# Gates one tick sooner, one product less in six pauses, and a last output block finished transposed

## The chip, the core and the metric

The kernel runs on one core of one Trainium2 chip. The metric is the device time of one execution in microseconds, the median of several runs. The engines are TensorE (PE: matrix products; PEld: its weight loads), VectorE (DVE), ScalarE (ACT), GpSimd (POOL) and SyncE (SP); DMA queues are fed by SP, ACT and POOL.

## The reference

A decoder trunk of two layers on 256 tokens of width 2048, all in float32. Layer 0 mixes by gated linear attention, layer 1 by sliding-window attention with sinks, and each mixer is followed by an MLP whose hidden width is 8192:

```python
def sqrelu_mlp(h, w1, w2):
    u = jax.nn.relu(h @ w1)
    return (u * u) @ w2

log_a = jax.nn.log_sigmoid((glr @ w_g2 + b_g).astype(f32)) / GLA_GATE_TAU
bc = jnp.cumsum(to_chunks(log_a, dk), axis=-2)
...
decay = jnp.exp(jnp.where(causal, diff, -jnp.inf))
attn = jnp.einsum('bhid,bhjd,bhijd->bhij', qi, ki, decay)
...
h = h + mixer(rmsnorm(h, norm_mix[layer]))
h = h + sqrelu_mlp(rmsnorm(h, norm_mlp[layer]), mlp_w1[layer], mlp_w2[layer])
```

The last line quotes the two updates of a layer in short; `mixer` stands for either of the two.

## The kernel before

Every weight block of 512 x 512 comes by a DMA into a tile (`ws`, `wx` or `wy`, 128 x 4 x 512) and is split by `halve` into a high half `wh` (a cast on ScalarE, L114) and a low half `wl` (a subtraction on VectorE, L115), each in two pieces of 128 x 1024. A product then takes, for each of four k, three matrix products: high activations by `wh`, high by `wl`, low by `wh`. The activations were split in the same way before. The residual stream lies in four tiles `xs[c]` of 512 columns with the tokens on the partitions, in two halves t of 128 tokens.

Python code emits the instructions, and a tile scheduler with priorities (`tc.high_priority`) orders each engine's instructions. Within the emission there is a calendar: `later(n, fn)` puts a piece of work n ticks ahead, and each chunk of a large product calls `tick()`.

In layer 0 the calendar spreads the gate computation over the large products. `gate` (four calls, a half hh of the columns and a half t of the tokens each) makes log_a; `cumsum` (four calls from tick `CS` on) its running sums by products with a triangular matrix; `levels(hp, n)` starts, for each pair of heads hp, the Gram products of seven levels (64, 32, ... 1) of the decay's blocks. A level computes its factors on VectorE (L582, L590), GpSimd and ScalarE into a tile `mlev`, and two ticks later `level_gram` multiplies them on PE into a bank of the two `ms` banks, from which VectorE's masked copy L604 takes the result. `diag(hp)` does the same for the diagonal products (`ms<-qT,kTt`), with the masked copy L614.

An MLP runs in four quarters g of the hidden width. In each, products with w1 fill the activations, and then `seven` forms the product with w2 for n = 0 and n = 1, in a scheme that replaces eight block products by seven of sums of blocks plus a few plain ones. Its names: `load` issues a weight block's DMA on SP; `more(x, i, j)` adds another block to tile x by an accumulating DMA on GpSimd (L1004); `product(b, o, ws)` splits `ws` and multiplies with operand o into bank b; `plain(i, j, b0, b1)` is a block product without a sum, one bank for each half of the tokens; `add` (L1041) and `sub` (L1042) bring banks into v or `xs`. At the very end (g = 3, n = 1 of the last MLP) `send(c, t, b, k)` transposes columns of `xs[c]` on PE (L1050), copies them on ScalarE (L1052) and issues the DMA to the output (L1053), which is stored with the tokens on the fast axis. `c0` and `c1` are the column blocks 2 and 3 there; `x11, x21` are the two halves of tokens of c0, `x12, x22` those of c1.

`pause` (L950 to L954) is called by the calendar once in each quarter and issues fp32 products of `ident` by a column of `ones` into an `ms` bank; its result is not used.

Of the kernel before, what the change touches and what calls it, by code (L numbers as in the profile page):

```python
# [16 lines left out]
P = 128  # L17
T = 256
NT = T // P
D = 2048  # L20
KT = D // P
C = 512
# [11 lines left out]
WS = 3  # L34
WHL = 4
WPRI = 60
QPRI = 100
LV = 2
WARM = 11
CS = 14  # L40
RS = 4
MX = 2
COMB = (1, 3)
# [6 lines left out]
def yoco_kernel(ctx: ExitStack, tc: tile.TileContext, x, norms, mlp_w1, mlp_w2, a_w_in, w_glr, w_gate, a_g_o, a_w_o,  # L50
                kv_w_k, kv_w_v, kv_g_k, b_w_q, b_g_q, b_sinks, b_w_o, out):
    nc = tc.nc
# [4 lines left out]
    wp = ctx.enter_context(tc.tile_pool(name="wp", bufs=2))  # L57
# [5 lines left out]
    def bank(shape, tag, dtype=F32):  # L63
        return ps[tag].tile(shape, dtype, name=tag, tag=tag)
# [7 lines left out]
    def later(n, fn):  # L72
        due.setdefault(now[0] + n, []).append(fn)

    def tick():
        now[0] += 1
        for fn in due.pop(now[0], ()):
            fn()

    def mm(o, l, r, start=True, stop=True, **kw):  # L80
        nc.tensor.matmul(o, lhsT=l, rhs=r, start=start, stop=stop, **kw)  # L81
# [23 lines left out]
    def halve(ws, o=C, n=2):  # L105

        whs = [wp.tile([P, 2, C], F32R, name="wh", tag="wh", bufs=WHL) for _ in range(2)]
        wl = wp.tile([P, 4, C], F32R, name="wl", tag="wl", bufs=WS)
        with tc.high_priority(offset=WPRI):
            for k in range(0, 4, n):  # L110
                wh = whs[k // 2]
                js, ks = slice(k % 2, k % 2 + n), slice(k, k + n)
                w = ws[k // 2] if isinstance(ws, list) else ws[:, ks, :o]
                nc.scalar.copy(out=wh[:, js, :o], in_=w)  # L114
                nc.vector.tensor_sub(out=wl[:, ks, :o], in0=w, in1=wh.bitcast(F32)[:, js, :o])  # L115
        return [(whs[k // 2][:, k % 2], wl[:, k]) for k in range(4)]
# [98 lines left out]
    class Seven:  # L215
# [16 lines left out]
        def load(self, i, j):  # L232
            ws = wp.tile([P, 4, C], F32, name="ws", tag="ws", bufs=WS)
            with tc.high_priority(offset=WPRI):
                nc.sync.dma_start(out=ws, in_=self.block(i, j))
            return ws
# [28 lines left out]
        def plain(self, i, j, b0, b1):  # L265
            halves = halve(self.load(i, j))
            ps_ = [self.use(b) for b in (b0, b1)]
            for k in range(4):
                wh, wl = halves[k]
                for t in range(NT):  # L270
                    p, st = ps_[t]
                    a, l = self.token(i, t)
                    mm(p, a[:, k], wh, st and k == 0, False, skip_group_check=True)
                    mm(p, a[:, k], wl, False, False, skip_group_check=True)
                    mm(p, l[:, k], wh, False, k == 3, skip_group_check=True)
                if k % 2:
                    tick()
# [90 lines left out]
    tail, last = {}, []  # L368
# [175 lines left out]
    def gate(t, hh):  # L544
        cs = slice(hh * C, (hh + 1) * C)
        zp = bank([P, C], "ms")
        for i, w in enumerate((wgh, wgl)):
            mm(zp, zin[:, t * P:(t + 1) * P], w[:, cs], i == 0, i == 1)
        e = g2.tile([P, C], F32, name="e", tag="og")
        nc.scalar.activation(out=e, in_=zp, func=AF.Abs)  # L550
        nc.scalar.activation(out=e, in_=e, func=AF.Exp, scale=-1.0)
        nc.scalar.activation(out=e, in_=e, func=AF.Ln, bias=1.0)
        nc.vector.scalar_tensor_tensor(out=la[t][:, cs], in0=zp, scalar=0.0, in1=e, op0=ALU.min, op1=ALU.subtract)
# [109 lines left out]
    glr(bank([P, 2, T], "tp"), 5)  # L663
    for hh in range(2):
        for t in range(NT):
            later(7 + 4 * hh + 2 * t, lambda t=t, hh=hh: gate(t, hh))
    for c2 in range(4):
        later(CS + c2, lambda c2=c2: cumsum(c2))
    go_all(gemm_q(0))
# [269 lines left out]
    def mlp(w1, w2, act, r, gains):  # L939
# [7 lines left out]
        wide_tags.sort()  # L947
        vs = [mp.tile([P, C], F32, name=f"v{n}", bufs=1) for n in range(2)]

        def pause():  # L950

            pt = small()
            for i in range(2):
                mm(pt[:, i:i + 1], ident, ones[:, 0:1])  # L954

        def new_ops():
# [29 lines left out]
        def seven(w, n, op, us, g, acts, gains, sq, nr):  # L986
# [21 lines left out]
            def use(b):  # L1008
                if b in banks:
                    return banks[b], False  # L1010
                banks[b] = bank([P, C], "ms" if b in "EF" else "acc")
                return banks[b], True

            def product(b, o, ws):
                p, st = use(b)
                halves = halve(ws)
                for k in range(4):
                    wh, wl = halves[k]
                    mm(p, op[o][:, 0, k], wh, st and k == 0, False, skip_group_check=True)
                    mm(p, op[o][:, 0, k], wl, False, False, skip_group_check=True)  # L1020
                    mm(p, op[o][:, 1, k], wh, False, k == 3, skip_group_check=True)
                tick()
                return p
# [20 lines left out]
            def send(c, t, b=0, k=4, queue=nc.scalar if n == 0 else nc.sync):  # L1044

                if c not in left:
                    left[c] = mp.tile([P, 4, T], F32, name="xt", tag="u")
                tp = bank([P, 4, P], ("tp", "ms")[t * n])
                for j in range(k):
                    nc.tensor.transpose(out=tp[:, j, :], in_=xs[c][:, t, (b + j) * P:(b + j + 1) * P], identity=ident)  # L1050
                o, r, tt = left[c][:, b:b + k, t * P:(t + 1) * P], c * C + b * P, slice(t * P, (t + 1) * P)
                nc.scalar.copy(out=o, in_=tp[:, :k])  # L1052
                queue.dma_start(out=out[r:r + k * P, tt].rearrange("(k p) t -> p k t", p=P), in_=o)  # L1053

            def done(c):
# [10 lines left out]
                if len(turn) == NC4:  # L1066
                    later(1, lambda: rstd_of(nr, sq))


            x = load(mp, "wx", 2, 0, 0)  # L1070
            p = product("A", 0, x)
# [15 lines left out]
            with tc.high_priority(offset=WPRI):  # L1087
                nc.vector.tensor_add(out=y, in0=y, in1=b12)
            sub(x22, product("C", 6, y))
            for i in (2, 3):  # L1090
                plain(i, 0, "A", "C", i == 2)
            add(v, product("D", 5, x))
# [7 lines left out]
                nc.vector.tensor_add(out=x, in0=x, in1=b21)  # L1100
            product("A", 1, b21)
            add(x11, banks["A"])
            if g == n + 2 == 3 and not gains:

                p, _ = use("C")
                halves = halve(x)
                for b in range(2):
                    bs = slice(b * T, (b + 1) * T)
                    for k in range(4):
                        wh, wl = (w[:, bs] for w in halves[k])  # L1110
                        mm(p[:, bs], op[3][:, 0, k], wh, False, False, skip_group_check=True)
                        mm(p[:, bs], op[3][:, 0, k], wl, False, False, skip_group_check=True)
                        mm(p[:, bs], op[3][:, 1, k], wh, False, k == 3, skip_group_check=True)
                    tick()
                    add(x21[:, bs], p[:, bs])
                send(c0, 0)
                for b in range(2):
                    send(c0, 1, 2 * b, 2, nc.scalar)
                return
            add(x21, product("C", 3, x))  # L1120
            if g == 3:
                done(c0)
# [2 lines left out]
        for g in range(4):  # L1125
            w = w2[g * D:(g + 1) * D]
            us, op, uf = {}, None, {}
            later(1 if g else RS + 3, pause)
            for c in range(NC4):
                if c >= 2:  # L1130
                    us[c] = new_act()
                elif c == 0:
                    op = new_ops()
                ms = {}

                def evac_u(f, acc, c=c, ms=ms):
                    if f % 2 == 0:
                        ms[0] = mp.tile([P, 2, T], F32, name="m", tag="m")
                    if f == 0:
                        uf[c] = mp.tile([P, 4, T], F32, name="u", tag="u")  # L1140
                    m, j = ms[0], f % 2
                    nc.scalar.copy(out=m[:, j], in_=acc[:, 1])
                    nc.vector.tensor_add(out=m[:, j], in0=acc[:, 0], in1=m[:, j])
                    if j == 0:
                        return
                    bs = slice(f - 1, f + 1)
                    nc.vector.scalar_tensor_tensor(out=m, in0=m, scalar=0.0, in1=rb2, op0=ALU.max, op1=ALU.mult)
                    nc.scalar.activation(out=uf[c][:, bs], in_=m, func=AF.Square)
                    if c >= 2:
                        ah, al, _ = us[c]  # L1150
                        nc.scalar.copy(out=ah[:, bs], in_=uf[c][:, bs])
                        nc.vector.tensor_sub(out=al[:, bs], in0=uf[c][:, bs], in1=ah.bitcast(F32)[:, bs])
                    elif f == 3:
                        combine(op, c, uf)

                go_all(gemm_wide(piece(w1, g * D + c * C), act, evac_u))
            for n in range(2):
                seven(w, n, op, us, g, acts, gains, sq, nr)
# [241 lines left out]
```

## Time and profile before

| what | value |
|---|---|
| median of 3 runs | 2036.23 us (2035.28 to 2036.71) |
| the profiled execution, its own time | 2036.59 us |
| span in its profile | 2034.9 us |
| busy PE | 2023.3 us, 99% of the span |
| busy DVE | 1546.8 us, 76% |
| busy ACT | 1202.9 us, 59% |
| busy POOL | 161.4 us, 8% |
| granted TensorE clock over the span | 1.0 |

Busy time is the time in which at least one instruction of the engine is under way. The span is the time from the first to the last instruction that the profile shows; what lies around it is in the execution's own time alone. The granted clock is the share of full speed (2.4 GHz) that TensorE was given; 0.5 is its lower level of 1.2 GHz.

### The profile page before, as it was taken

What the parts mean: (1) busy time and instruction counts of PE and PEld (TensorE: products, weight loads), DVE (VectorE), ACT (ScalarE), POOL (GpSimd) and SP (SyncE); (2) the same over time, 40 slices, a digit from 0 to 9 for tenths busy, and PEclk for the clock granted to TensorE, in tenths of its full rate; (3) what the DMA queues carried; (4) which work ended last, traced back from release to release, by engine and by line L of the source; (5) the groups of instructions that cost most, each with busy time, mean ns of one, the idle gap of its engine ahead of it and who ended that gap; (6) DMA issues with size and microseconds to landing.
All of it is one profiled execution on the core that took longest, in us unless ns stands there. A gap on an engine that the chain in (4) does not pass through costs nothing.

```text
span 2034.9 us, 26993 instructions
## 1 busy us (share of the span) xinstructions
PE 2023.3 (99%) x10578; PEld 1716.3 (84%) x10578; DVE 1546.8 (76%) x1796; ACT 1202.9 (59%) x1638; POOL 161.4 (8%) x175
## 2 busy tenths in 40 slices
PE   9999999999999999999999999999999999999999
PEld 9988888888888888888887877788888888888887
DVE  6698787867866876786798676876876786787777
ACT  6746666656555655555566677655655555555555
POOL 2151110000000000000001121000000000000000
PEclk9999999999999999999999999999999999999999
DMA  8445876676965785776666543775785786687575
GB/s 287 160 140 179 224 207 207 188 255 179 267 229 190 225 267 186 213 242 228 186 207 188 166 145 123 200 258 186 227 264 191 200 255 218 188 255 230 186 224 148
DMA packets 219280, 423.15 MB, mean 208 GB/s; under 512 B 7328, under 2 KB 17840, under 8 KB 219152
## 3 DMA queue, kind: packets, MB, share of 16 engines
q1 hardware_dynamic: 194224, 376.59, 54.3%
q0 software_dynamic: 21568, 42.81, 12.2%
q10 hardware_dynamic: 3360, 2.01, 0.3%
q8 instruction: 83, 1.36, 0.3%
q14 instruction: 45, 0.37, 0.1%
HBM read 419.29 MB, written 2.10 MB: 207 GB/s over the span
## 4 chain that ended last, share of the span: by engine, by line
PE 91%; DVE 4%; ACT 2%; DMA 1%; issue 1%; POOL 0%; SPq 0%; ACTq 0%; DVEq 0%; POOLq 0%
PE acc L81 58%; PE ms L81 22%; PE tp L81 10%; DVE wl L115 1%; ACT sc L1283 1%; DMA ws<-in_a_w_in_dram 1%; DMA wx<-in_mlp_w_dram 1%; PE tp L831 0%; ACT wh L114 0%; DVE sc L1293 0%; PE tp L1215 0%; DVE st L1277 0%; DVE act L340 0%; PE tp L701 0%; DVE po L1310 0%
## 5 line engine op out<-in xcount | busy, mean ns | idle before, releaser
L115 DVE TENSOR_TENSOR wl<-ws,wh 128x1024 fp32r<-128x1024 f32 x600 | 737.7, 1238 | 277.9 <-ACT wh L114 274.6
L114 ACT CAST wh<-ws 128x1024 fp32r<-128x1024 f32 x600 | 629.0, 1052 | 448.9 <-PE acc L81 285.9
L81 PE MATMUL acc<-wh,act 128*128 128x512 f32 x1696 | 544.5, 394 | 0.5 <-DVE xs L1042 0.3
L81 PE MATMUL acc<-act,wh 128*128 128x512 f32 (+1 forms) x1536 | 453.7, 359 | 0.0
L81 PEld LDWEIGHTS acc<-wh,act 128*128 128x128 f32 x1696 | 317.5, 188 | 69.0 <-issue 2.0
L81 PE MATMUL acc<-act,wl 128*128 128x256 f32 x1280 | 355.1, 279 | 0.1
L81 PE MATMUL acc<-wl,act 128*128 128x512 f32 x848 | 330.2, 390 | 0.0
L81 PEld LDWEIGHTS acc<-act,wh 128*128 128x128 f32 x1536 | 272.6, 189 | 43.5
L115 DVE TENSOR_TENSOR wl<-wx,wh 128x1024 fp32r<-128x1024 f32 x160 | 193.5, 1222 | 87.6 <-ACT wh L114 85.2
L114 ACT CAST wh<-wx 128x1024 fp32r<-128x1024 f32 x160 | 167.9, 1054 | 143.4 <-PE acc L81 81.1
L81 PEld LDWEIGHTS acc<-act,wl 128*128 128x128 f32 x1280 | 241.3, 189 | 1.6 <-DVE wl L402 0.3
L81 PE MATMUL tp<-act,wh 128*128 128x512 f32 x528 | 204.6, 392 | 0.8 <-DVE wh L518 0.8
L81 PE MATMUL ms<-act,wh 128*128 128x512 f32 x512 | 202.0, 394 | 0.0
L81 PEld LDWEIGHTS acc<-wl,act 128*128 128x128 f32 x848 | 159.4, 188 | 32.8 <-issue 1.4
L81 PE MATMUL ms<-wh,act 128*128 128x512 f32 x512 | 163.4, 390 | 0.0
L81 PE MATMUL ms<-act,wl 128*128 128x256 f32 x512 | 143.4, 280 | 0.0
L1004 POOL DMA_DIRECT2D wx<-in_mlp_w_dram x32 | 41.2, 1288 | 1268.2 <-DVE wl L115 1252.5
L81 PE MATMUL tp<-act,wl 128*128 128x256 f32 x512 | 140.7, 275 | 0.0
L81 PE MATMUL acc<-wh,ops 128*128 128x512 f32 (+1 forms) x392 | 123.6, 386 | 0.3 <-ACT wh L114 0.3
L81 PE MATMUL acc<-wh,op 128*128 128x512 f32 x384 | 123.4, 389 | 0.0
L81 PEld LDWEIGHTS tp<-act,wh 128*128 128x128 f32 x528 | 99.1, 188 | 24.3 <-DVE wh L518 1.0
L81 PEld LDWEIGHTS ms<-act,wh 128*128 128x128 f32 x512 | 95.7, 187 | 21.6
(278 smaller groups left out, 2556.2 us busy)
## 6 DMA issues: line engine op xcount, KB each, us to landing
ws<-in_mlp_w_dram SPq DMA_DIRECT2D x224, 1024.0 KB, 5.3
ws<-in_a_w_in_dram SPq DMA_DIRECT2D x42, 1024.0 KB, 5.0
wx<-in_mlp_w_dram POOLq DMA_DIRECT2D x32, 1024.0 KB, 9.2
wx<-in_mlp_w_dram SPq DMA_DIRECT2D x16, 1024.0 KB, 5.1
wy<-in_mlp_w_dram SPq DMA_DIRECT2D x16, 1024.0 KB, 7.8
ws<-in_b_w_q_dram SPq DMA_DIRECT2D x16, 1024.0 KB, 5.0
ws<-in_a_w_o_dram SPq DMA_DIRECT2D x15, 1024.0 KB, 5.1
ws<-in_b_w_o_dram SPq DMA_DIRECT2D x15, 1024.0 KB, 5.0
```

Of the source, the lines that this page charges most:

```text
L81: nc.tensor.matmul(o, lhsT=l, rhs=r, start=start, stop=stop, **kw)
L114: nc.scalar.copy(out=wh[:, js, :o], in_=w)
L115: nc.vector.tensor_sub(out=wl[:, ks, :o], in0=w, in1=wh.bitcast(F32)[:, js, :o])
L1004: nc.gpsimd.dma_start(out=ws, in_=block(i, j).rearrange("(k p) n -> p k n", p=P), accum_op=ALU.add)
L1283: nc.scalar.activation(out=sc[:, h], in_=sc[:, h], func=AF.Exp, bias=nmx[:, h:h + 1], scale=f[:, h:h + 1], accum_out=su[:, h:h + 1])
```

## The change

Three edits. `CS` goes from 14 to 13 and the gates from tick 7 + ... to 6 + ..., so gates, running sums and the levels of the first pair of heads (they start at `CS - 6`) come one tick sooner; the levels of the second pair stay. `pause` takes a number and issues one product instead of two in quarters 1 to 3 of either MLP, two in quarter 0 as before. The last `seven` goes, after its product "C" 6, into the new function `last(x, y)`: it does plain(2, 0), the product "A" 1, the product "D" 5, plain(3, 0) for the first 256 of 512 columns only, and the product "C" 3, whose weight x + b21 is now formed in tile y. The last 256 columns of plain(3, 0) are computed by `turned(j)` with the weights as the stationary operand, so that the result comes with the columns on the partitions, 128 columns j by 256 tokens; the part of these columns that lies in `xs` is transposed beside it (L1115 after the change), copied, and the two are added (`leave`) and sent out.

```diff
-CS = 14
+CS = 13
...
-            later(7 + 4 * hh + 2 * t, lambda t=t, hh=hh: gate(t, hh))
+            later(6 + 4 * hh + 2 * t, lambda t=t, hh=hh: gate(t, hh))
...
-        def pause():
+        def pause(n):
 
             pt = small()
-            for i in range(2):
+            for i in range(n):
                 mm(pt[:, i:i + 1], ident, ones[:, 0:1])
...
+            def last(x, y):
+
+                plain(2, 0, "A", "C", True)
+                b21 = load(wp, "ws", WS, 1, 0)
+                product("A", 1, b21)
+                with tc.high_priority(offset=WPRI):
+                    nc.vector.tensor_add(out=y, in0=x, in1=b21)
+                add(v, product("D", 5, x))
+                add(x12, v)
+                add(x22, v)
+                done(c1)
+                sub(x21, v)
+                halves = halve(load(wp, "ws", WS, 3, 0))
+                ah, al, _ = us[3]
+                for t, b in enumerate("AC"):
+                    tt = slice(t * P, (t + 1) * P)
+                    for k in range(4):
+                        wh, wl = (w[:, :T] for w in halves[k])
+                        mm(banks[b][:, :T], ah[:, k, tt], wh, False, False, skip_group_check=True)
+                        mm(banks[b][:, :T], ah[:, k, tt], wl, False, False, skip_group_check=True)
+                        mm(banks[b][:, :T], al[:, k, tt], wh, False, k == 3, skip_group_check=True)
+                    tick()
+                add(x11, banks["A"])
+                p = product("C", 3, y)
+                for bs in (slice(T, C), slice(0, T)):
+                    add(x21[:, bs], p[:, bs])
+                send(c0, 0, 0, 2)
+                xt = left[c0]
+
+                def turned(j):
+
+                    pt = bank([P, T], "acc")
+                    for k in range(4):
+                        wh, wl = (w[:, j * P:(j + 1) * P] for w in halves[k])
+                        mm(pt, wh, ah[:, k], k == 0, False)
+                        mm(pt, wl, ah[:, k], False, False)
+                        mm(pt, wh, al[:, k], False, k == 3)
+                    return pt
+
+                def leave(j, pt, queue):
+                    add(xt[:, j], pt)
+                    queue.dma_start(out=out[c0 * C + j * P:c0 * C + (j + 1) * P, :], in_=xt[:, j])
+                p2 = turned(2)
+                tp = bank([P, 2, T], "tp")
+                for j in range(2):
+                    for t in range(NT):
+                        nc.tensor.transpose(out=tp[:, j, t * P:(t + 1) * P], in_=xs[c0][:, t, T + j * P:T + (j + 1) * P],
+                                            identity=ident)
+                nc.scalar.copy(out=xt[:, 2:], in_=tp)
+                leave(2, p2, nc.sync)
+                send(c0, 1, 0, 2, nc.scalar)
+                leave(3, turned(3), nc.sync)
...
+            if g == n + 2 == 3 and not gains:
+                last(x, y)
+                return
             for i in (2, 3):
                 plain(i, 0, "A", "C", i == 2)
             add(v, product("D", 5, x))
...
-            if g == n + 2 == 3 and not gains:
...
-            later(1 if g else RS + 3, pause)
+            later(1 if g else RS + 3, lambda n=1 if g else 2: pause(n))
```

How the change moves instructions shows in two places. The first is VectorE at the end of the program, in the last `seven`; `wl<-ws` is the low half of a plain block or of b21, `wl<-wx` that of x, `wl<-wy` that of y. Before:

```order
L115 TENSOR_TENSOR wl<-wy,wh 128x1024
L115 TENSOR_TENSOR wl<-ws,wh 128x1024
L1041 TENSOR_TENSOR xs<-acc,xs 128x512
L115 TENSOR_TENSOR wl<-ws,wh 128x1024 x2
L1042 TENSOR_TENSOR xs<-xs,acc 128x512
L115 TENSOR_TENSOR wl<-ws,wh 128x1024
L115 TENSOR_TENSOR wl<-wx,wh 128x1024 x2
L1100 TENSOR_TENSOR wx<-wx,ws 128x2048
L115 TENSOR_TENSOR wl<-ws,wh 128x1024 x2
```

and now:

```order
L115 TENSOR_TENSOR wl<-wy,wh 128x1024
L1075 TENSOR_TENSOR wy<-wx,ws 128x2048
L115 TENSOR_TENSOR wl<-ws,wh 128x1024 x4
L1041 TENSOR_TENSOR xs<-acc,xs 128x512
L1042 TENSOR_TENSOR xs<-xs,acc 128x512
L115 TENSOR_TENSOR wl<-wx,wh 128x1024 x2
L115 TENSOR_TENSOR wl<-ws,wh 128x1024 x2
L115 TENSOR_TENSOR wl<-wy,wh 128x1024 x2
```

The sum x + b21 (L1100 before, L1075 now) has moved from behind the two `wl<-wx` to the place ahead of all four `wl<-ws`. Of these four the first two are plain(2, 0)'s in both; the last two were plain(3, 0)'s and are now b21's.

The second is PE in the gate stretch, from the diagonal products of the second pair of heads (`ms<-qT,kTt`) on; `ms<-mlev` are the Gram products of a level, `acc<-wh,act` and `acc<-wl,act` the large product's chunks of twelve. Before:

```order
L81 MATMUL ms<-qT,kTt 128x128 x8
L81 MATMUL ms<-mlev 128x128 x4
L81 MATMUL acc<-wh,act 128x512
L81 MATMUL acc<-wl,act 128x512
L81 MATMUL acc<-wh,act 128x512 x2
L81 MATMUL acc<-wl,act 128x512
L81 MATMUL acc<-wh,act 128x512 x2
L81 MATMUL acc<-wl,act 128x512
L81 MATMUL acc<-wh,act 128x512 x2
L81 MATMUL acc<-wl,act 128x512
L81 MATMUL acc<-wh,act 128x512
L81 MATMUL ms<-mlev 128x128 x4
```

and now:

```order
L81 MATMUL ms<-qT,kTt 128x128 x8
L81 MATMUL acc<-wh,act 128x512
L81 MATMUL acc<-wl,act 128x512
L81 MATMUL acc<-wh,act 128x512 x2
L81 MATMUL acc<-wl,act 128x512
L81 MATMUL acc<-wh,act 128x512 x2
L81 MATMUL acc<-wl,act 128x512
L81 MATMUL acc<-wh,act 128x512 x2
L81 MATMUL acc<-wl,act 128x512
L81 MATMUL acc<-wh,act 128x512
L81 MATMUL ms<-mlev 128x128 x8
```

The four Gram products that stood right behind the diagonal ones have moved behind the next chunk of twelve, where they stand together with the four of the other pair of heads.

## Rows read from the trace of the kernel before

**Rows 1.** The page: the span, TensorE's line of part 1 (busy time, share of the span, instructions) and the chain that ended last by engine.

```profile
span 2034.9 us, 26993 instructions
...
PE 2023.3 (99%) x10578; PEld 1716.3 (84%) x10578; DVE 1546.8 (76%) x1796; ACT 1202.9 (59%) x1638; POOL 161.4 (8%) x175
...
PE 91%; DVE 4%; ACT 2%; DMA 1%; issue 1%; POOL 0%; SPq 0%; ACTq 0%; DVEq 0%; POOLq 0%
```

**Rows 2.** The waits of PE from 120 to 150 us: engine, line, what it waited for, us in total, times, longest.

```profile
PE ms L81 <- DVE AT L614: 0.9, 1, 0.9
```

**Rows 3.** PE's timeline in the gate stretch. Columns here and in the other timelines: start in us, us, engine, line, operation, out<-in, tile, shapes, count, and in brackets the idle time before and what ended it.

```profile
128.18 1.95 PE L81 MATMUL ms<-qT,kTt 128*128 128x128 f32 x16
...
133.36 0.39 PE L81 MATMUL acc<-wh,act 128*128 128x512 f32 x1
134.63 1.13 PE L81 MATMUL ms<-mlev 128*128 128x128 f32 x8 [0.88 <-DVE AT L614]
135.52 0.47 PE L81 MATMUL acc<-wh,act 128*128 128x512 f32 x1
```

**Rows 4.** VectorE's timeline in the gate stretch.

```profile
131.82 1.98 DVE L115 TENSOR_TENSOR wl<-ws,wh 128x1024 fp32r<-128x1024 f32 x1 [0.25 <-ACT wh L114]
133.72 0.76 DVE L614 COPY_PREDICATED AT<-ident,ms 128x256 f32<-128x256 int32 x2
```

**Rows 5.** PE's timeline around the pause of quarter 1 of the first MLP.

```profile
581.19 0.28 PE L81 MATMUL acc<-act,wl 128*128 128x256 f32 x1
581.31 0.50 PE L81 MATMUL ms<-ones,ident 128*128 128x1 f32 x4
581.67 0.48 PE L81 MATMUL acc<-act,wh 128*128 128x512 f32 x1
581.98 0.28 PE L81 MATMUL acc<-act,wl 128*128 128x256 f32 x1
582.10 0.63 PE L81 MATMUL acc<-act,wh 128*128 128x512 f32 x2
```

**Rows 6.** VectorE's timeline at the same place.

```profile
581.04 0.69 DVE L1041 TENSOR_TENSOR xs<-acc,xs 128x512 f32<-128x512 f32 x1
```

**Rows 7.** All instructions that read the tile `ones`, grouped, the pauses' line: count, then duration in ns (least, median, most), first and last start.

```profile
L81 PE MATMUL ms<-ones,ident x32: 164/250/250, 427.1 to 1858.6; 128*128 128x1 f32 x32
```

**Rows 8.** VectorE's timeline at the end of the program.

```profile
2005.29 1.22 DVE L115 TENSOR_TENSOR wl<-wy,wh 128x1024 fp32r<-128x1024 f32 x1 [0.30 <-ACT wh L114]
2006.65 1.23 DVE L115 TENSOR_TENSOR wl<-ws,wh 128x1024 fp32r<-128x1024 f32 x1
...
2017.43 2.29 DVE L1100 TENSOR_TENSOR wx<-wx,ws 128x2048 f32<-128x2048 f32 x1
2019.64 1.22 DVE L115 TENSOR_TENSOR wl<-ws,wh 128x1024 fp32r<-128x1024 f32 x1
...
2030.57 0.42 DVE L1041 TENSOR_TENSOR xs<-acc,xs 128x256 f32<-128x256 f32 x1 [1.85 <-PE acc L81]
```

**Rows 9.** GpSimd's timeline at the end of the program: the accumulating DMA's issue.

```profile
2001.37 1.28 POOL L1004 DMA_DIRECT2D wx<-in_mlp_w_dram  x1 [13.82 <-DVE wl L115]
```

**Rows 10.** The instructions on the tile `wx` from 1990 us on: the time from the DMA's issue to its landing.

```profile
DMA to landing us min/median/max: 11.2/11.2/11.2
```

**Rows 11.** PE's timeline at the end of the program.

```profile
2009.44 0.39 PE L81 MATMUL acc<-wh,act 128*128 128x512 f32 x1
2009.67 0.39 PE L81 MATMUL acc<-wl,act 128*128 128x512 f32 x1
...
2025.87 0.28 PE L81 MATMUL acc<-wl,ops 128*128 128x256 f32 x1
...
2027.07 0.28 PE L81 MATMUL acc<-wh,ops 128*128 128x256 f32 x1
2027.19 0.60 PE L1050 MATMUL tp<-ident,xs 128*128 128x128 f32 x4
2027.63 0.60 PE L1050 MATMUL ms<-ident,xs 128*128 128x128 f32 x4
...
2031.14 0.41 PE L1050 MATMUL ms<-ident,xs 128*128 128x128 f32 x2 [0.39 <-DVE xs L1041]
```

**Rows 12.** ScalarE's timeline at the end of the program (ACTq is its DMA queue).

```profile
2013.72 1.05 ACT L114 CAST wh<-wx 128x1024 fp32r<-128x1024 f32 x1 [3.02 <-PE acc L81]
...
2031.61 0.37 ACT L1052 COPY xt<-ms 128x256 f32<-128x256 f32 x1 [0.45 <-PE ms L1050]
2032.01 0.38 ACTq L1053 DMA_DIRECT2D out_dram<-xt  x1
```

**Rows 13.** Stretches at the very end: window, its length, busy time of PE, PEld, DVE, ACT and POOL (instructions), granted clock, DMA share, GB/s.

```profile
2034.60:2034.70 0.10, 0.00 (x0) 0.00 (x0) 0.00 (x0) 0.00 (x0) 0.00 (x0) 1.00 0.00 0
2034.70:2034.80 0.10, 0.00 (x0) 0.00 (x0) 0.00 (x0) 0.00 (x0) 0.00 (x0) 0.58 0.00 0
2034.80:2034.90 0.10, 0.00 (x0) 0.00 (x0) 0.00 (x0) 0.00 (x0) 0.00 (x0) 0.50 0.00 0
```

**Rows 14.** PE's timeline at the start of the program.

```profile
1.20 5.06 PE L81 MATMUL ms<-ones 128*128 128x128 f32 x22 [1.20 <-POOL ones L89]
6.08 1.71 PE L81 MATMUL acc<-act,wh 128*128 128x256 f32 x8
7.63 0.64 PE L81 MATMUL acc<-act,wl 128*128 128x256 f32 x4
8.10 0.40 PE L81 MATMUL acc<-act,wh 128*128 128x256 f32 x2
```

More of the change, by code (lines that the diff above doesn't have):

```diff
@@ L1102, in seven @@
             add(x11, banks["A"])
-            if g == n + 2 == 3 and not gains:
[L1105 to L1119, printed above, removed]
             add(x21, product("C", 3, x))
```

## The prediction

> **What bounds the kernel now.** I read the page first. TensorE is busy for 99% of the span and holds 91% of the chain that ended last [rows 1]. So a change can gain in two ways only: it takes work off PE, or it closes one of the few gaps in PE's row. It loses wherever it opens a gap. Then I read the three places of the change in the timelines of PE and of the engine that PE follows there: the gate stretch of layer 0 (126 to 142 us), one pause (581 us), and the end (2001 to 2035 us). The reader should see in each who arrives last.
>
> In the gate stretch PE waits once: the Gram product at 134.63 should have followed the product of 133.36 after 0.23 us, comes after 1.27, and is released by the masked copy L614 [rows 2, 3]. VectorE was in a 1.98 us group of L115 and started L614 only at 133.72, for 0.76 us [rows 4]. So that gap is about 1.04 us long.
>
> A pause is four records (an fp32 product leaves two) at 581.31. They push the next product to 581.67 [rows 5].
>
> At the end PE has no gap from 2009.44 to 2027.19; the products of 512 columns are 0.227 us apart (72 of them before 2025.76) and those of 256 columns 0.12 (2025.87 to 2027.07 is ten steps) [rows 11]. VectorE is ahead of PE there: at 2006.65 it makes the first low half (`wl<-ws`) that PE takes at 2009.67 [rows 8, 11]. So DVE leads by some 1.8 us once that half is finished, 2006.65 + 1.23 = 2007.88. That lead is the cover on which the tail's new order rests.
>
> **Gates one tick sooner.** Nothing is added or removed. The levels of the two halves now fall on the same ticks, so the order of Gram products around the diagonal product changes (the second excerpt above). The Gram product that follows the diagonal one after twelve products takes the bank that a level's L604 frees, and L614's bank is taken only by the second Gram product, 0.8 us later (8 records of 134.63 fill 0.89 up to 135.52) [rows 3]. L614 itself still stands behind an L115 on DVE [rows 4]. I take 0.85 us of the 1.04 as gained; the bounds are 0 (L614 comes that much later too) and 1.04 (the gap goes).
>
> **One product less in six pauses.** Eight pauses left 32 records [rows 7]; six of them lose two records each. 581.31 to 581.67 is 0.36 us for four records, so two are 0.18 us, and six times that is 1.1 us [rows 5]. The cover: the products behind the pause need a bank that the add of 581.04 frees at 581.73, and the one that takes it is the second of the pair at 582.10, at about 582.33 [rows 5, 6]; that leaves 0.6 us, and 0.4 after the change, so no wait comes up. Bounds: 0 (the bank's wait takes the place) to 1.4 (the delay of the product behind, 581.67 to 581.98 instead of 0.23, shrinks as well).
>
> **The tail's work.** Before, PE did from 2009.44 on 72 products of 512 columns, 24 of 256 and 16 transposes; after, 60 of 512, 48 of 256 and 16 transposes. With the rows' steps (0.227, 0.12, and 0.11 for a transpose, 2027.19 to 2027.63 for four [rows 11]) this is 13.6 + 5.8 + 1.8 = 21.1 us, and PE's last product would stand finished at about 2030.8. An add of 0.42 us as at 2030.57 [rows 8] and a DMA follow, so the last DMA issues near 2031.25. Before, the last transposes at 2031.14, an ACT copy at 2031.61 and the DMA at 2032.01 came last [rows 11, 12]. Gain 0.75 us, between 0.2 (a wait like the one before 2031.14 comes back) and 0.9.
>
> **The tail's order on VectorE.** This is the term that decides. `y = x + b21` (L1075) now stands right behind the last `wl<-wy` and ahead of all four `wl<-ws` of plain(2,0) and b21 (first excerpt). It reads x, the `wx` tile to which POOL adds a block by an accumulating DMA, issued at 2001.37 and 11.2 us on its way [rows 9, 10]. So it lands at 2012.57. VectorE is free at 2005.29 + 1.22 = 2006.5 [rows 8], and takes its instructions in the order given: it sits at L1075 for 6 us. Behind it are queued the low halves that PE needs at once. In the kernel before, the same tile was read first at 2013.72, by ACT, released by PE [rows 12], so the transfer was hidden.
>
> The sum there: landing 2012.57, L1075 takes 2.21 until the next may start (2017.43 to 2019.64 for L1100, the same size), L115 takes 1.23 [rows 8]: 2016.0. PE wanted that half at 2009.67 [rows 11], so PE idles 6.35 us. Bounds: 5.8 (landing 0.55 sooner) and 7.4 (the ACT cast of 2013.72, released with 0.3 us lead by PE, only shows that x was there by 2013.6, about 1.05 later than I take). Once restarted, DVE needs 1.2 us a piece where PE needs 1.36 (six products), so it leads again; only L1042, behind four L115 now, frees a bank about 0.1 us late (0 to 0.3).
>
> **TensorE's clock after the gap.** After PE's last transposes (2031.14 + 0.41 = 2031.55) the granted clock is 1.00 for 3.2 us and falls to 0.58 and then 0.50, the 1.2 GHz level, in 2034.70 to 2034.90 [rows 11, 13]. PE's new gap is about 6 us long (2010.06 to 2016.0), so the clock should fall inside it. How long PE stays slow after it is not shown for a gap of this size; the nearest row is the program's start. There PE begins at 1.20 and runs 256-column products 0.19 us apart on the mean from 6.08 to 7.63, and 0.12 from 7.63 to 8.10 [rows 14]: some 6.3 us at half pace, in which 3.15 us of work is lost. Bounds 0 (the clock doesn't fall) and 3.2 (as at the start); given that it falls I take 1.6 to 3.2, in the middle 2.4.
>
> The Trainium skill speaks against this change here: its page "TensorE: Matmul & The Clock Gate", section "HAM oscillation — how this bites in real kernels", says that a wait for a DMA between blocks of products can throttle TensorE again, so that the next block starts at the half clock. By that rule the tail costs the wait and the slow restart; without it the wait alone.
>
> **Sum.** −0.85 (gates) − 1.1 (pauses) − 0.75 (tail's end) + 6.35 (gap) + 0.1 (bank) + 2.4 (clock) = +6.15 us. The profiled execution took 2036.59 us (span 2034.9 and 1.7 around it), so 2042.7; it is 0.36 above the median 2036.23, against which I forecast 2042.4. A measurement of this kernel can tell about 0.2%, 4.07 us: the bounds are 2032.2 and 2040.3.
>
> **Rivals.**
> (B) *The gap comes, the clock stays.* Then +3.75: 2040.0, which is within 0.2%. For it: the fall at the end came only after 3.2 us of idling, and PE's gap may be shorter if x lands sooner. Against: 6 us is nearly twice 3.2 [rows 13]. The point from which it decides is a gap under about 3.2 us, that is x landing before about 2009.5.
> (C) *No gap to speak of: the accumulating DMA lands in time.* Then L1075 could start when DVE is free, at 2006.5, and PE's half is ready at 2006.5 + 2.21 + 1.23 = 2009.95, 0.3 us late: −0.85 − 1.1 − 0.75 + 0.3 = −2.4, that is 2033.8, not slower. It needs x by 2006.5, 5.1 us after its issue; the row says 11.2 [rows 10]. Less traffic beside it would have to halve it. Even with every gain at its bound (1.04 + 1.4 + 0.9 = 3.3) this is no gain over 0.2%.
> (D) *Gates and pauses give nothing* (the bank waits take their place) while the gap stays: +8.1, 2044.3. The slack of 0.4 us behind the pause speaks against it [rows 5, 6].
>
> **How the numbers follow.** Gap with a slow restart, my forecast: 0.73, its own range 2040.8 to 2044.0. (B) 0.13. (C) 0.08. (D) and other slower ends 0.06. Slower: 0.73 less a little that ends under 2040.3, plus 0.06: 0.76. Within 0.2%: (B) and most of (C): 0.21. Faster, a (C) with gains I can't see: 0.03. The range leaves out (C), the low part of (B) and the top of (D): 2039.6 to 2044.2.
>
> **What would show it.** Right: in the DVE row of the tail L1075 starts at about 2010 to 2011 (2 us sooner than 2012.57 through the gains ahead) after some 6 us of idling; PE has a gap of 6 us after the first product of plain(2,0), released by DVE L115; the granted clock falls to 0.5 in or behind it. The gate stretch shows no wait over 0.5 us for L614, and pauses show two records, 0.18 us shorter. Wrong: L1075 starts within 3 us of the `wl<-wy` ahead of it; or PE's gap is covered because a transfer of x takes some 6 us; or products behind the gap are 0.23 us apart at once.

## The result, and the profile after

The changed kernel takes 2042.26 us (median of 7 runs, 2041.41 to 2044.16) where the kernel before takes 2035.98 (7 runs, 2034.83 to 2036.71): ratio 1.0031, 95% interval 1.0022 to 1.0040. It is 6.28 us slower. The forecast was 2042.4 us, slower.

The head of the page after: the span, and the busy times.

```profile
span 2039.7 us, 26992 instructions
...
PE 2023.7 (99%) x10578; PEld 1717.7 (84%) x10578; DVE 1548.0 (76%) x1798; ACT 1202.5 (59%) x1638; POOL 162.4 (8%) x175
```

PE's busy time is nearly that of before, and the span is 4.8 us longer than in [rows 1] (the profiled execution is the shortest of the seven, 2041.41 us). So PE does no more work; it stands still. VectorE's timeline at the end of the program shows who makes it stand:

```profile
2002.22 1.23 DVE L115 TENSOR_TENSOR wl<-wy,wh 128x1024 fp32r<-128x1024 f32 x1 [0.30 <-ACT wh L114]
2009.99 2.29 DVE L1075 TENSOR_TENSOR wy<-wx,ws 128x2048 f32<-128x2048 f32 x1 [6.54 <-DMA wx<-in_mlp_w_dram]
2012.20 4.63 DVE L115 TENSOR_TENSOR wl<-ws,wh 128x1024 fp32r<-128x1024 f32 x4
```

After the last `wl<-wy` DVE idles 6.54 us, and the profile names the releaser: the DMA into `wx`. L1075 starts at 2009.99, and only at 2012.20 do the four low halves follow that were at work from 2006.65 on in [rows 8]. The transfer itself, from issue to landing, on the tile `wx` from 1990 us on:

```profile
DMA to landing us min/median/max: 11.6/11.6/11.6
```

PE's timeline of the same stretch (its first product of plain(2,0) is at 2006.38; it was at 2009.44 in [rows 11]):

```profile
2006.38 0.39 PE L81 MATMUL acc<-wh,act 128*128 128x512 f32 x1
2013.48 0.80 PE L81 MATMUL acc<-wl,act 128*128 128x512 f32 x1 [6.71 <-DVE wl L115]
2014.07 1.05 PE L81 MATMUL acc<-wh,act 128*128 128x512 f32 x2
...
2017.43 0.39 PE L81 MATMUL acc<-wl,act 128*128 128x512 f32 x1
2017.66 0.40 PE L81 MATMUL acc<-wh,act 128*128 128x512 f32 x1
```

The second product comes 7.1 us behind the first, where 0.23 is usual. Nine products from 2013.48 to 2017.43 then take 3.95 us, 0.59 the first and some 0.42 each of the others; from 2017.43 on they are 0.23 apart again. The windows beside it (length, busy time of PE, PEld, DVE, ACT and POOL with instruction counts, granted clock, DMA share, GB/s) show the clock of this stretch:

```profile
2009.00:2010.00 1.00, 0.00 (x0) 0.00 (x0) 0.01 (x1) 0.00 (x0) 0.00 (x0) 1.00 0.03 6
2010.00:2011.00 1.00, 0.00 (x0) 0.00 (x0) 1.00 (x1) 0.00 (x0) 0.00 (x0) 0.77 0.00 0
2011.00:2013.00 2.00, 0.00 (x0) 0.00 (x0) 2.00 (x2) 0.00 (x0) 0.00 (x0) 0.50 0.00 0
2013.00:2017.00 4.00, 3.52 (x8) 2.81 (x9) 4.00 (x5) 0.00 (x0) 0.00 (x0) 0.50 0.00 0
2017.00:2018.00 1.00, 1.00 (x5) 0.80 (x4) 1.00 (x2) 0.00 (x0) 0.00 (x0) 0.82 0.00 0
2018.00:2019.00 1.00, 1.00 (x6) 0.82 (x5) 0.02 (x1) 0.00 (x0) 0.00 (x0) 1.00 0.00 0
```

The granted clock falls in the idle stretch to 0.50, the 1.2 GHz level, stays there through the first products and comes back to 1.00 within the window 2017 to 2018.

In the gate stretch the wait of 0.88 us for L614 [rows 2, 3] is gone from PE's row, but two double groups of Gram products have become long:

```profile
128.84 1.95 PE L81 MATMUL ms<-qT,kTt 128*128 128x128 f32 x16
130.53 0.48 PE L81 MATMUL acc<-wh,act 128*128 128x512 f32 x1
...
133.36 2.18 PE L81 MATMUL ms<-mlev 128*128 128x128 f32 x16
135.29 0.48 PE L81 MATMUL acc<-wh,act 128*128 128x512 f32 x1
...
140.83 2.31 PE L81 MATMUL ms<-mlev 128*128 128x128 f32 x16
142.90 0.48 PE L81 MATMUL acc<-wh,act 128*128 128x512 f32 x1
```

Sixteen records take 1.69 us where nothing holds them (128.84 to 130.53); the two pairs take 1.93 and 2.07. VectorE's masked copies at the same place point to the cause:

```profile
133.50 0.77 DVE L614 COPY_PREDICATED AT<-ident,ms 128x256 f32<-128x256 int32 x2
...
141.39 0.48 DVE L604 COPY_PREDICATED AT<-mask,ms 128x128 f32<-128x128 int32 x2
```

In the trace the ninth record of the first double group starts at 134.41, 0.14 us after L614 is finished (133.50 + 0.77), and that of the second at 142.02, 0.15 us after L604 is (141.39 + 0.48). Before, the group that the profile says was released by L614 started at the same distance from it (134.49 and 134.63). So PE seems still to wait there for a bank that VectorE empties, only shorter than the list of waits shows.

Earlier, the first gate's product no longer follows the product ahead of it by 0.12 us:

```profile
52.19 0.28 PE L81 MATMUL acc<-act,wh 128*128 128x256 f32 x1
52.53 0.47 PE L81 MATMUL ms<-wgh,zin 128*128 128x512 f32 x1
```

It comes 0.34 us after it: VectorE finishes its operand `zin` (L533) at 52.39. And a pause is now two records that push the next product by 0.14 us instead of the 0.36 of [rows 5]:

```profile
580.33 0.28 PE L81 MATMUL ms<-ones,ident 128*128 128x1 f32 x2
580.47 0.48 PE L81 MATMUL acc<-act,wh 128*128 128x512 f32 x1
```

### The profile page after: what moved, and what is told of

Read it like the earlier page. It is cut to its first block, busy times and chain, and to the rows that moved or that the text cites. A ratio compares the mean times of both kernels' runs of the same rounds, so it can differ in the third digit from the quotient of the medians.

```text
span 2039.7 us, 26992 instructions
## 1 busy us (share of the span) xinstructions
PE 2023.7 (99%) x10578; PEld 1717.7 (84%) x10578; DVE 1548.0 (76%) x1798; ACT 1202.5 (59%) x1638; POOL 162.4 (8%) x175
## 5 line engine op out<-in xcount | busy, mean ns | idle before, releaser
L81 PE MATMUL acc<-wl,act 128*128 128x512 f32 (+1 forms) x848 | 330.2, 390 | 6.7 <-DVE wl L115 6.7
L81 PE MATMUL acc<-wh,ops 128*128 128x512 f32 x384 | 123.3, 391 | 0.3 <-ACT wh L114 0.3
```

## The experiments

The theory: the whole loss is at the end, and its cause is the place of the sum x + b21 (L1075) on VectorE, ahead of low halves that PE needs, while it waits for a transfer; the clock adds to it; the other edits gain. The rivals: the early edits lose, or the transposed finish and the new order of the products cost time by themselves.

**The early edits alone**, on the kernel before, whose end stays:

```diff
-CS = 14
+CS = 13
...
-            later(7 + 4 * hh + 2 * t, lambda t=t, hh=hh: gate(t, hh))
+            later(6 + 4 * hh + 2 * t, lambda t=t, hh=hh: gate(t, hh))
...
-            later(1 if g else RS + 3, pause)
+            later(1 if g else RS + 3, lambda n=1 if g else 2: pause(n))
```

> Gates one tick sooner and one product in the six later pauses, with the end of the kernel before. Theory 1 (the whole loss is at the end, the first two edits gain): about 2 to 3 us under the kernel before, a ratio of 0.9985 to 0.9990, PE's product of 2009.44 comes some 2.5 to 3 us sooner, as in the changed kernel (3.06), and the wait for L614 is gone. Rival (part of the loss is in the early edits): not below before.

Measured: 2034.92 us against 2036.17, ratio 0.9992 (0.9983 to 1.0001), 1.25 us less. The interval just reaches 1, but all eleven runs (2034.00 to 2035.79) lie under the median of before, so the rival is unlikely; the gain is smaller than I expected. The expectation rested on the first profile of the changed kernel, whose first product of plain(2,0) came 3.06 us sooner; here it comes 1.05 sooner (2008.39). Half of that 3.06 has nothing to do with the change. The product `ms<-ones,wx` at the start, ahead of all three edits, stands at 43.48 us before, 42.79 in the first profile after (0.69 sooner) and 44.67 here (1.19 later). From the last quarter of the first MLP to the first of the second, where no edit lies, the profile of before takes 422.67 us, the first one after 421.86 and this one 421.83; the other seven lie between 421.43 and 422.19. What is left of the 3.06 is 0.28 us up to the first pause and 1.28 in the six quarters with one product less.

**The new end alone**, on the changed kernel, whose gates and pauses go back:

```diff
-CS = 13
+CS = 14
...
-            later(6 + 4 * hh + 2 * t, lambda t=t, hh=hh: gate(t, hh))
+            later(7 + 4 * hh + 2 * t, lambda t=t, hh=hh: gate(t, hh))
...
-            later(1 if g else RS + 3, lambda n=1 if g else 2: pause(n))
+            later(1 if g else RS + 3, lambda n=2: pause(n))
```

> The new end alone, on the gates and pauses of before. Theory 1: PE idles some 6.5 us at the second product of plain(2,0) behind L1075, the clock falls, and the kernel is 7.5 to 9.5 us above before (ratio 1.0037 to 1.0047). Rival (the end costs only part of it): under 5 us.

Measured: 2043.88 us, ratio 1.0035 (1.0023 to 1.0048), 7.7 us more. The loss is all in the end; with the −1.25 of the run before it makes +6.45, near the 6.28 of the whole change. VectorE and PE show the same picture:

```profile
2011.37 2.29 DVE L1075 TENSOR_TENSOR wy<-wx,ws 128x2048 f32<-128x2048 f32 x1 [6.17 <-DMA wx<-in_mlp_w_dram]
```

```profile
2008.12 0.39 PE L81 MATMUL acc<-wh,act 128*128 128x512 f32 x1
2014.86 0.80 PE L81 MATMUL acc<-wl,act 128*128 128x512 f32 x1 [6.34 <-DVE wl L115]
```

DVE idles 6.17 us for the transfer, and PE's second product is 6.74 us behind the first.

**The sum later.** The one line that decides, undone by a dependency: the sum goes into b21's own tile, which the four low halves must have read first.

```diff
                 with tc.high_priority(offset=WPRI):
-                    nc.vector.tensor_add(out=y, in0=x, in1=b21)
+                    nc.vector.tensor_add(out=b21, in0=x, in1=b21)
...
-                p = product("C", 3, y)
+                p = product("C", 3, b21)
```

> As the changed kernel, but the sum x + b21 goes into the tile of b21 instead of y, which keeps it behind the four low halves that read plain(2,0) and b21. Theory 1 (the loss is L1075's place on VectorE): no gap in PE, the clock stays at 1.00, and all three edits gain: 2.7 to 4 us under before (ratio 0.9980 to 0.9987). Rival (the transposed finish or the new order of the products costs time by itself): at or above before.

Measured: 2033.67 us, ratio 0.9987 (0.9978 to 0.9996): 2.5 us faster than before, where the changed kernel was 6.28 slower. VectorE, then PE:

```profile
2005.04 1.22 DVE L115 TENSOR_TENSOR wl<-ws,wh 128x1024 fp32r<-128x1024 f32 x1
...
2006.79 2.35 DVE L115 TENSOR_TENSOR wl<-ws,wh 128x1024 fp32r<-128x1024 f32 x2
...
2009.65 1.22 DVE L115 TENSOR_TENSOR wl<-ws,wh 128x1024 fp32r<-128x1024 f32 x1
2011.06 2.29 DVE L1075 TENSOR_TENSOR ws<-wx,ws 128x2048 f32<-128x2048 f32 x1 [0.19 <-DMA wx<-in_mlp_w_dram]
```

```profile
2007.84 0.39 PE L81 MATMUL acc<-wh,act 128*128 128x512 f32 x1
2008.06 0.39 PE L81 MATMUL acc<-wl,act 128*128 128x512 f32 x1
...
2028.95 0.28 PE L81 MATMUL acc<-act,wh 128*128 128x256 f32 x1
```

The low halves go first, L1075 waits 0.19 us for the same transfer (11.2 us here too), and PE goes on after 0.22 us. From the first product of plain(2,0) to the end of the span it takes 24.56 us (2007.84 to 2032.4), where before took 25.46 (2009.44 to 2034.9). The three other profiles with the old end take 25.4 to 25.5, the other one with the late sum 24.6. So the transposed finish and the new order gain 0.9 us, and the second rival falls.

**The sum behind three of the four.** It goes into a new tile of the `ws` pool, and the scheduler leaves one piece of b21's low half behind it:

```diff
+                w30 = load(wp, "ws", WS, 3, 0)
+                y = wp.tile([P, 4, C], F32, name="ws", tag="ws", bufs=WS)
                 with tc.high_priority(offset=WPRI):
                     nc.vector.tensor_add(out=y, in0=x, in1=b21)
...
-                halves = halve(load(wp, "ws", WS, 3, 0))
+                halves = halve(w30)
```

> As the changed kernel, but the sum goes into a new tile behind three of the four low halves, with one piece of b21's low half left behind it. Theory 1: PE's gap shrinks to about 2.5 us and moves to the middle of product A 1. If the clock then stays at 1.00, the kernel is within 1 us of before (gap 2.5, edits -3); if it falls as after the long gap, 1.5 to 2 us above before. Rival (position doesn't matter): as the changed kernel, 6 us above.

Measured: 2036.49 us, ratio 1.0002 (0.9993 to 1.0011). The gap has shrunk and moved into the product "A" 1, as PE's timeline and the windows show:

```profile
2010.78 0.61 PE L81 MATMUL acc<-wh,ops 128*128 128x512 f32 x2
2014.04 0.50 PE L81 MATMUL acc<-wl,ops 128*128 128x512 f32 x1 [2.64 <-DVE wl L115]
2014.37 0.62 PE L81 MATMUL acc<-wh,ops 128*128 128x512 f32 x2
2014.83 0.40 PE L81 MATMUL acc<-wh,act 128*128 128x512 f32 x1
```

```profile
2012.00:2013.00 1.00, 0.00 (x0) 0.00 (x0) 1.00 (x2) 0.25 (x1) 0.00 (x0) 1.00 0.00 0
2013.00:2014.00 1.00, 0.00 (x0) 0.00 (x0) 1.00 (x2) 0.00 (x0) 0.00 (x0) 1.00 0.00 0
2014.00:2015.00 1.00, 0.96 (x4) 0.84 (x5) 1.00 (x2) 0.00 (x0) 0.00 (x0) 1.00 0.00 0
```

PE idles 2.64 us, the granted clock stays at 1.00, and the products are 0.33 and then 0.23 us apart. The end takes 27.48 us (2006.92 to 2034.4), 2.92 more than with the late sum. So the place on VectorE sets the gap, and this gap costs its own length, 2.81 us from the place where the product was due, and no slow restart.

**The gates alone.**

```diff
-CS = 14
+CS = 13
...
-            later(7 + 4 * hh + 2 * t, lambda t=t, hh=hh: gate(t, hh))
+            later(6 + 4 * hh + 2 * t, lambda t=t, hh=hh: gate(t, hh))
```

> Gates one tick sooner alone. Theory: the one gap of 1.04 us at the Gram product behind L614 closes, 0.6 to 1.04 us under before (ratio 0.9995 to 0.9997), and PE is 0.8 to 1.0 us sooner at the first pause. Rival (the gap moves to another Gram product): no change at the first pause.

Measured: 2035.76 us against 2036.05, ratio 0.9999 (0.9990 to 1.0008). PE is not sooner at the first pause (427.45), since this execution also began late. Measured from `ms<-ones,wx` to the first pause, which leaves the start out, it takes 383.26 us here, 383.31 in the first profile of the changed kernel, and 383.59 before; the mean of all seven profiles with the sooner gates is 383.38 (383.26 to 383.65), that of the three without 383.54. So the gates are worth about 0.2 us by the profiles, whose ranges overlap, and nothing that the runs can tell; the rival is nearer to the truth. Where the 1.04 us went is in PE's row, the same two double groups as after:

```profile
134.69 2.23 PE L81 MATMUL ms<-mlev 128*128 128x128 f32 x16
...
142.21 2.28 PE L81 MATMUL ms<-mlev 128*128 128x128 f32 x16
```

**The pauses alone.**

```diff
-        def pause():
+        def pause(n):
...
-            for i in range(2):
+            for i in range(n):
...
-            later(1 if g else RS + 3, pause)
+            later(1 if g else RS + 3, lambda n=1 if g else 2: pause(n))
```

> One product in the six later pauses alone. Theory: 0.21 us for each, 1.3 us under before (ratio 0.9994). Rival (the bank's wait takes the place): no step at the pauses, ratio 1.0000.

Measured: 2034.87 us, ratio 0.9994 (0.9986 to 1.0003), 1.2 us less, which the runs alone can't tell from nothing; the profile can. From the pause of quarter 1 to that of quarter 2 it is now 170.66 us (581.62 to 752.28), 170.87 before (581.31 to 752.18): 0.21 a pause, and no wait in its place.

```profile
581.62 0.28 PE L81 MATMUL ms<-ones,ident 128*128 128x1 f32 x2
```

**No product in the six pauses**, on top of the late sum:

```diff
-            pt = small()
+            pt = small() if n else None
...
-            later(1 if g else RS + 3, lambda n=1 if g else 2: pause(n))
+            later(1 if g else RS + 3, lambda n=0 if g else 2: pause(n))
```

> As the kernel with the late sum, and no product at all in the six later pauses. If a product costs 0.21 us here too: 1.3 us under the late sum, 4 to 5 us under before (ratio 0.9976 to 0.9980). Rival (without any pause PE waits for the bank that VectorE's add frees): a wait of PE for L1041 at the six places and no further gain.

Measured: 2033.35 us, ratio 0.9987 (0.9978 to 0.9996), 0.3 us under the late sum, which this measurement can't tell from nothing. In the profile a quarter of the second MLP takes 170.42 us (from the first product on an `op` operand to that of the next quarter, 1617.86 to 1788.28) and 170.66 with one product (1618.21 to 1788.87), so here too a product is worth 0.2 us and no wait for L1041 comes up. Part of why the total did not show it is in this execution: the first quarter of its first MLP took 172.04 us by the same rows (513.07 to 685.11) and the second 170.44, without a wait that the profile names and with the granted clock at 1.00.

What is slower there is the pace of PE. Each w1 product of 512 columns by `wh` is followed by one of 256 columns by `wl`. Two rows of this run, eighteen such pairs apart, and two of the run with the late sum, seventeen apart, all behind the place of the pause:

```profile
583.62 0.40 PE L81 MATMUL acc<-act,wh 128*128 128x512 f32 x1
...
589.98 0.40 PE L81 MATMUL acc<-act,wh 128*128 128x512 f32 x1
```

```profile
583.78 0.39 PE L81 MATMUL acc<-act,wh 128*128 128x512 f32 x1
...
589.67 0.40 PE L81 MATMUL acc<-act,wh 128*128 128x512 f32 x1
```

A pair takes 0.353 us here and 0.346 there. PE starts each quarter's w1 products at the slower pace, and behind a pause it goes on at the quicker one. In this stretch it stayed at the slower pace for 240 pairs, which makes the 1.6 us. With one or two products in the pause none of the 54 such quarters in the other nine profiles did that; without any, one of six did. So the pause's products may be worth more than they cost, although their result is not used; one such quarter does not show it. What sets the pace is open, and so is whether it makes the spread of these eleven runs (2031.49 to 2035.29).

**The changed kernel once more**, unaltered.

> The changed kernel once more, for a second profile: its times spread over 2041.4 to 2044.2. If the spread is the slow restart, the gap before it stays at 6.4 to 6.9 us and the half-clock stretch behind it has another length than the 3.9 us of the first profile; if it is the transfer, the landing of x moves.

Measured: 2041.59 us, one run. PE's timeline:

```profile
2007.15 0.39 PE L81 MATMUL acc<-wh,act 128*128 128x512 f32 x1
2013.34 0.79 PE L81 MATMUL acc<-wl,act 128*128 128x512 f32 x1 [5.81 <-DVE wl L115]
...
2017.77 0.47 PE L81 MATMUL acc<-wh,act 128*128 128x512 f32 x1
2018.07 0.40 PE L81 MATMUL acc<-wh,ops 128*128 128x512 f32 x1
```

Both moved. The transfer took 10.7 us instead of 11.6, and the second product comes 5.96 us late (2007.15 + 0.23 to 2013.34) instead of 6.87. The slow stretch lasts from 2013.34 to 2018.07, 4.73 us for eleven products, in place of 3.95 for nine. So neither of the two expectations alone holds: transfer and restart both vary, and in this pair they went against each other. Both profiled executions lie at the short end of the 2041.4 to 2044.2, so what makes the longer ones is not shown.

## Why the prediction was right, step by step

- **The order on VectorE** (forecast: 6.35 us of idle PE). PE lost 6.87, 5.96 and, with the new end alone, 6.51 us there; the mean is 6.45. L1075 started at 2009.99, at the edge of the forecast stretch of 2010 to 2011, partly because this execution ran ahead from its start. The landing that I took from one transfer of before (11.2 us) was 11.6, 10.7 and 11.2, so the row carried over although it belongs to a kernel in which nobody waited for that transfer.
- **The clock** (forecast 2.4, between 1.6 and 3.2). Nine products in 3.95 us instead of 2.04 are 1.91 us lost; eleven in 4.73 instead of 2.49 are 2.24, twice (the other time with the new end alone, 2014.86 to 2019.59). The value was nearer to the lower bound, which was half of the loss at the start and had no row of its own. Rival (B), the gap with the clock unchanged, falls for this gap, and the run with a gap of 2.64 us shows that it would have held for a short one. This bears out the Trainium skill, page "TensorE: Matmul & The Clock Gate", section "HAM oscillation — how this bites in real kernels", where it says that a wait for a DMA can throttle TensorE again: the first products behind the 6.7 us of idling ran at 0.50, and those behind 2.64 us at 1.00.
- **The tail's work** (forecast −0.75): −0.9, from the run with the late sum. From the first product of plain(2,0) to the end of PE's last one it takes 21.4 us, as forecast (2007.84 to 2028.95 + 0.28 there, 2009.44 to 2030.8 in the forecast); the rest is what follows PE.
- **The bank behind L1042** (forecast 0.1): none. Gap and slow restart of the first profile, 6.87 + 1.91 = 8.78, leave nothing of the 33.32 − 24.56 = 8.76 us by which its tail (2006.38 to 2039.7, its last product below) is longer than with the late sum.

```profile
2036.22 0.28 PE L81 MATMUL acc<-act,wh 128*128 128x256 f32 x1
```

- **The pauses** (forecast −1.1): 0.21 to 0.22 us each, 1.3 in all. Four records push the next product by 0.36 us and two by 0.14, so the two that go are worth more than the half that I took; the bound of 1.4 held it. I took a pause for pure cost; in the run without its products one quarter of six kept the slower pace, 1.6 us longer, so that may not be all.
- **The gates** (forecast −0.85): this step failed in its size. I took 0.85 of the 1.04 us "as gained". The wait of 0.88 us is gone, but where the Gram products of both pairs of heads share their ticks, the second half of the group seems to wait for the bank that L614 or L604 empties on VectorE: 0.24 and 0.38 us over 1.69 for the two groups. The first gate waits 0.22 us for its operand. Together 0.84 of the 1.04 come back, and 0.2 remain. The lower bound of 0 held, and had named just this (L614 comes later too); I then counted on the 0.8 us of the group's first half as cover. It was 0.16 us too short at L614, and I had not looked at the next pair or at the gate.

By the measured sizes the sum is −0.2 − 1.3 − 0.9 + 6.45 + 2.1 = +6.15 us; the medians differ by 6.28. That this is also the sum that I forecast is luck in part: the gates gave 0.65 less than I took, pauses and the tail's work 0.35 more, and gap, bank and clock together cost 0.3 less, which cancels.

Rival (C), the transfer in time, fell with its first row: 11.6 us, not 5. That less traffic beside it could have halved its time is unlikely, as the DMA queue of this transfer alone shows in the first profile after, from 1998.3 to 2002.3 us and from there to 2010 (packets, MB, share of the 16 DMA engines):

```profile
q0 software_dynamic: 5, 0.01, 3.5%
```

```profile
q0 software_dynamic: 523, 1.04, 74.8%
```

In the first 4 us behind its issue almost nothing of it moves, while the other queues move 1.5 MB; its own bytes then take some 7 us, most of them with no other transfer under way. That second part alone is longer than the 5.1 us that (C) allowed from issue to landing.

Rival (D), nothing from gates and pauses, was half true: true of the gates.

## What to carry to other kernels

An instruction with a high priority that waits for a transfer is as costly as everything queued behind it on its engine: look in the order of the engine for what stands behind, take the landing from the trace, and count until the first of those instructions could run. A slow transfer that no one waits for is not visible in the chain of waits, but its row is there, and it becomes the bound as soon as a reader is moved ahead of it. Where the order can't be given directly, a dependency can do it: writing the result into a tile that the urgent instructions still read turned a loss of 6.3 us into a gain of 2.5.

## What the runs showed of the hardware that was not expected

A transfer of 1 MB with addition took 10.7 to 11.6 us in all ten profiles. Its first packet came 3.7 to 4.2 us after its issue, and its packets then took 6.6 to 7.4 us; why it starts so late is open. The stretch in which products are slow after the long idle differs from one execution to the next (3.95, 4.73 and 4.73 us at the same place of the program), and so does the gap itself. Whether the changed kernel's times spread more for it is not shown: its seven runs lie within 2.8 us, those of before within 1.9 here and within 2.6 in the 27 runs beside the first four experiments. And TensorE ran the same w1 products at two paces, 0.353 and 0.346 us a pair, with the same granted clock of 1.00.
